# Last FFN projection of a decoder layer: lighter forms for three pairs, weight sums in two goes, another order at its start and its end

## The chip, the cores and the metric

The kernel runs on one core of a Trainium2 chip. The time is the device time of one execution in microseconds (us). TensorE (PE in the profile, PEld its weight loads) multiplies, VectorE (DVE) and ScalarE (ACT) work on the elements, GpSimd (POOL) helps, SyncE (SP) issues most transfers.

## The reference

One layer over 512 tokens of width 1024, in fp32:

```python
h = rms_norm(x, norm_mix)
q_a, k_a, v_a, u_b, gate_b, gate_c, g_a, g_b = split(h @ w_in)
o_a = stick_breaking_attention(q_a, k_a, v_a)           # 8 heads of 64, causal
y_b = gate_b * causal_depthwise_conv(gate_c * u_b, conv_w)
x = x + (sigmoid(g_a) * (o_a @ w_branch_a) + sigmoid(g_b) * (y_b @ w_branch_b)) @ w_mix_out
x = x + memory_cross_attention(rms_norm(x, norm_mem_q), rms_norm(mem, norm_mem_kv), ...)   # 256 memory tokens
gate, up = split(rms_norm(x, norm_ffn) @ w_ffn_in)      # 2 x 2816 columns
x = x + (silu(gate) * up) @ w_ffn_out
out = rms_norm(x, norm_final)
```

## The kernel before

Activations stand transposed, channels on the 128 partitions and tokens along the row. Every fp32 product is made of three fp32r products: a tile is split into a high part (an ACT cast, names ending in h) and the rest (a DVE subtraction, names ending in l), and TensorE adds high by high, high by rest and rest by high. A weight goes through `wr` (loaded), `wh` and `wl`.

The stages come one after another: input projection, attention and convolution, branches and merge (`merged`), the split of the memory; its keys (`km`, `kml`) and values (`vm`); the output projection of the mixer with its residual (`residual`, bank `r`, tiles `x1` and their gained split `x1g`); the memory attention; then the two FFN projections.

Both FFN projections use seven block products in place of eight (the Winograd form of Strassen's scheme). In the first one (`uses`, with bank names z, v and y), the tile m of the 22 hidden tiles gets products 0 to 6; `reads` and `second` bring them out of PSUM; `evict(m, 0..2)` multiplies by the scale `r2b`, takes the silu on ACT and writes the result into `acts[j]`, j being the pair of two hidden tiles, 11 in all (NJ), with two row blocks and two token halves in each.

The last projection (matmuls into `p`) needs per pair the forms of the activations, `forms[i, j]`, and of the weights, `ows[i, j]`, for i = 0 to 6. `act_first` makes forms 0 and 1 (cast f01h), `act_second` the forms 2 and 6 in one cast of 128x512 (f26h), form 3 (from n2) and t34, a 128x512 operation that prepares 4 and 5 in place; `act_third` makes 4 and 5 (f45h). The weights of products 0, 1 and 5 come from the matrix itself; those of 2, 3 and of 4, 6 are sums of its blocks, which POOL makes ahead, during the earlier stages: `weight_sums` loads a pair's four blocks (`pre`), adds four times, and stores the result to DRAM (`sums`). It starts behind `merged[1]`, whose element POOL copies first to be held back; its pool `prepool` must be closed before the FFN's pool `fpool` opens.

The projection runs in two loops. The first one makes products 0 to 3 of every pair: `run(i, j)` is product i of pair j, two token tiles of 128 with three matmuls each; between them `part()` takes the next entry of `first_parts`, which writes the casts and subtractions of a pair to come. Entries for the first two or three pairs are written inside the last products of the first projection. The second loop makes products 4, 6 and 5 and, in between, turns eight blocks of the residual (`turned`, `begin`, `onto`: `rt` and `nrt` are the scales by token and their negative). Then come the closing matmuls, the squares for the final norm (`square`), the multiplication by the gain (`gained` on POOL), `rstd` with `rstd_end` (a Newton step for the reciprocal root after Ln and Exp), and the stores.

On PE, ACT and DVE this part runs in the order in which it is written (`manual_schedule`); POOL and SP take their queues in order as well.

Of the kernel before, what the change touches and what calls it, by code (L numbers as in the profile page):

```python
# [34 lines left out]
SUMS_AT = 1  # L35

# [4 lines left out]
def hybrid_layer(ctx: ExitStack, tc: tile.TileContext, xT_d, memT_d, cols_d, wv_d, win_d,  # L41
# [414 lines left out]
    def weight_sums(prepool):  # L456

        for j in range(NJ):
            t = prepool.tile([P, 4, 512], F32, tag="pre", name=nm("pre"))
            if j < 2:  # L460
                nc.gpsimd.tensor_copy(t[:, 0, 0:1], f(merged[SUMS_AT][0])[:, 0:1])
            nc.gpsimd.dma_start(t, wfo_d[j])
            for a, b in ((0, 2), (2, 1), (1, 0), (3, 1)):
                nc.gpsimd.tensor_tensor(out=t[:, a, :], in0=t[:, a, :], in1=t[:, b, :], op=ALU.add)  # L464
# [129 lines left out]
    x1, x1g, mean1 = residual(wmix_d, merged, None, g_q)  # L594

# [205 lines left out]
    def act_first(j):  # L801
        for i, (hi, lo) in enumerate(zip(*map(halves, split(acts[j][0], "f01")))):
            forms[i, j] = hi, lo

    def act_second(j):

        n1, b22 = halves(acts[j][1])
        n2 = tmp("n2", HS)
        nc.vector.scalar_tensor_tensor(out=n2, in0=n1, scalar=-1.0, in1=b22, op0=ALU.mult,
                                       op1=ALU.subtract)  # L810
        for i, (hi, lo) in zip((2, 6), zip(*map(halves, split(acts[j][1], "f26")))):
            forms[i, j] = hi, lo
        hi, lo = halves(unit("f3"))
        nc.scalar.copy(hi, n2)
        nc.vector.tensor_tensor(out=lo, in0=n2, in1=f(hi), op=ALU.subtract)
        forms[3, j] = hi, lo
        b = acts[j][0].rearrange("p (i t) -> p i t", i=2)
        nc.vector.scalar_tensor_tensor(out=b, in0=n2[:, None, :].broadcast_to([P, 2, HS]),
                                       scalar=-1.0, in1=b, op0=ALU.mult, op1=ALU.subtract)

    def act_third(j):
        for i, (hi, lo) in zip((4, 5), zip(*map(halves, split(acts[j][0], "f45")))):
            forms[i, j] = hi, lo

    def out_pair(j, src, i0, i1):
# [4 lines left out]
        nc.scalar.copy(hi, raw)  # L830
        nc.vector.tensor_tensor(out=lo, in0=raw, in1=f(hi), op=ALU.subtract)  # L831
        for n, i in enumerate((i0, i1)):
            ows[i, j] = hi[:, n, :], lo[:, n, :]

    def out_one(j):
# [7 lines left out]
        nc.vector.tensor_tensor(out=w[:, 1, :], in0=raw, in1=f(w[:, 0, :]), op=ALU.subtract)  # L843
# [4 lines left out]

    first_parts = []
    for j in (0, 1):  # L850
        first_parts.append(lambda j=j: (out_pair(j, wq(j), 0, 1), act_first(j)))
    for j in (0, 1):
        first_parts.append(lambda j=j: (out_pair(j, sums[j][:, 0:2, :], 2, 3), act_second(j)))
    for j in range(2, NJ - 2):
        first_parts.append(lambda j=j: (out_pair(j, wq(j), 0, 1), act_first(j)))
        first_parts.append(lambda j=j: (out_pair(j, sums[j][:, 0:2, :], 2, 3), act_second(j)))
    for j in (NJ - 2, NJ - 1):
        first_parts.append(lambda j=j: (out_pair(j, wq(j), 0, 1), act_first(j)))
    for j in (NJ - 2, NJ - 1):
        first_parts.append(lambda j=j: (out_pair(j, sums[j][:, 0:2, :], 2, 3), act_second(j)))  # L860
# [5 lines left out]
    with tc.manual_schedule(engines={mybir.EngineType.PE, mybir.EngineType.Activation,  # L866
# [6 lines left out]
        for n, (m, i) in enumerate(uses):  # L873
# [36 lines left out]

# [20 lines left out]
        for j in (0, 1):  # L931
            run(0, j)
            part()
            run(1, j)
        res[3] = [ztile("p3") for _ in range(2)]
        res[2] = [otile("p2") for _ in range(2)]
        for j in (0, 1):
            run(2, j)
            part()
            run(3, j)  # L940
        for j in range(2, NJ - 2):
# [5 lines left out]
            run(3, j)  # L947
        last = NJ - 2, NJ - 1
# [13 lines left out]
        out_pair(0, sums[0][:, 2:4, :], 4, 6)  # L962
# [4 lines left out]
        out_pair(1, sums[1][:, 2:4, :], 4, 6)  # L967
        out_one(0)

        res[4], res[6] = [ztile("p4") for _ in range(2)], [mmtile("p6") for _ in range(2)]  # L970
        gain = [f(unit("gain")) for _ in range(2)]
        for h in range(2):
            nc.sync.dma_start(gain[h], gfin_d[:, h * 512:(h + 1) * 512].broadcast_to([P, 512]))
        ss = cpool.tile([P, 2 * TT], F32, tag="ss", name="ss")
# [46 lines left out]
        for j in range(NJ - 2):  # L1021
# [7 lines left out]
            out_pair(j + 2, sums[j + 2][:, 2:4, :], 4, 6)  # L1029
            if j > 0:  # L1030
# [6 lines left out]
        out_one(NJ - 1)  # L1037
        for s2 in range(2):
# [42 lines left out]
        def end(s2):  # L1081
            for j in range(NJ - 3, NJ):
                run(5, j, [s2])
            onto(ys[s2, 1], res[5][s2], s2, ys[s2, 1], -1)
            square(s2, 1)

        hi, t0, t1 = slice(2, 4), slice(0, 1), slice(1, 2)
        rstd(hi)
        end(0)
        rstd_end(hi)  # L1090
        store(2, 1, "act")
        store(2, 0, "dve")
        rstd(t0)
        end(1)
        store(3, 1, "act")
        rstd_end(t0)
        store(0, 1, "both")
        store(0, 0, "act")
        rstd(t1)
        store(3, 0, "dve")  # L1100
# [66 lines left out]
```

## Time and profile before

| | |
|---|---|
| three runs | 867.35, 867.08, 866.11 us (median 867.08) |
| the profiled execution | 869.89 us, its span 868.2 us |
| mean granted clock of TensorE | 0.993 |
| PE busy | 850.9 us, 98% of the span, 4840 matmuls |
| PEld busy | 739.7 us, 85% |
| DVE busy | 659.8 us, 76%, 1080 instructions |
| ACT busy | 460.5 us, 53%, 842 |
| POOL busy | 153.1 us, 18%, 183 |

A row of the timeline gives the start within the span and the duration in us, the engine and the line of the kernel, the operation with what it writes and reads (an arrow from the inputs to the output), the sizes, and in brackets how long the engine had been idle and what released it. The profiled execution is one of its own, 2.81 us above the median of the three runs, with 1.69 us lying outside its span; rows and sums of rows are measured against it.

### The profile page before, as it was taken

Reading aid. Unit: us, or ns where it says so; the run is one execution under the profiler, and the core shown is the slowest. Engines: PE = TensorE matmul, PEld = TensorE weight load, DVE = VectorE, ACT = ScalarE, POOL = GpSimd, SP = SyncE. Lnnn points to the kernel's source line nnn. Section 1 sums busy time; section 2 is a strip of 40 time slices with the busy share of each in tenths; the row PEclk is TensorE's granted clock in tenths of the full one; section 3 lists DMA queues with packets and bytes.
Section 4 is the critical chain, followed back from the end, with each engine's and each line's share of the span. In section 5 each row is a group of like instructions: output and inputs, shape, how many; then the busy total and the mean of one; then the engine's idle time right before and its main releaser. Section 6 shows DMA issues by size and latency. Waiting matters only on the chain.

```text
span 868.2 us, 12834 instructions
## 1 busy us (share of the span) xinstructions
PE 850.9 (98%) x4840; PEld 739.7 (85%) x4840; DVE 659.8 (76%) x1080; ACT 460.5 (53%) x842; POOL 153.1 (18%) x183
## 2 busy tenths in 40 slices
PE   9999999999999999999999999999999999899995
PEld 7878888887888888888888789999999999788884
DVE  7768888987665778656555679888778887798866
ACT  7566676775332344443344556644555555566545
POOL 0021221101666665100000001111111110000002
PEclk9999999999999999999999999999999999899998
DMA  8332222224677788733341435777777763365642
GB/s 292 121 110 85 85 64 70 77 76 165 229 282 294 283 317 315 243 97 97 121 111 49 108 75 140 177 183 183 182 193 185 183 170 107 102 225 190 212 136 97
DMA packets 48574, 139.54 MB, mean 161 GB/s; under 512 B 4608, under 2 KB 6656, under 8 KB 45696
## 3 DMA queue, kind: packets, MB, share of 16 engines
q1 hardware_dynamic: 39008, 103.82, 35.7%
q0 software_dynamic: 9216, 34.61, 15.5%
q8 instruction: 38, 0.62, 0.3%
q10 hardware_dynamic: 288, 0.28, 0.1%
q14 instruction: 24, 0.20, 0.1%
HBM read 125.07 MB, written 13.63 MB: 160 GB/s over the span
## 4 chain that ended last, share of the span: by engine, by line
PE 92%; DVE 4%; issue 2%; ACT 1%; DMA 1%; SPq 0%; POOL 0%; DVEq 0%; ACTq 0%; POOLq 0%
PE z L724 14%; PE p L919 10%; PE pr L151 8%; PE pr L152 8%; PE pr L153 8%; PE y L724 7%; PE v L724 4%; PE r L152 3%; PE r L151 3%; PE r L153 3%; PE v L257 2%; PE br L151 2%; PE mq L153 2%; PE mq L151 2%; PE mq L152 2%
## 5 line engine op out<-in xcount | busy, mean ns | idle before, releaser
L146 ACT CAST wh<-wr 128x1024 fp32r<-128x1024 f32 x84 | 88.1, 1052 | 159.0 <-issue 66.9
L147 DVE TENSOR_TENSOR wl<-wr,wh 128x1024 fp32r<-128x1024 f32 x84 | 116.2, 1387 | 34.5 <-ACT wh L146 34.3
L152 PE MATMUL pr<-xgl,wh 128*128 128x512 f32 x288 | 112.5, 390 | 0.0
L151 PE MATMUL pr<-xgh,wh 128*128 128x512 f32 x288 | 112.4, 390 | 0.0
L153 PE MATMUL pr<-xgh,wl 128*128 128x512 f32 x288 | 112.2, 390 | 0.0
L693 POOL DMA_DIRECT2D ws<-in_w_ffn_in_dram x22 | 26.5, 1206 | 315.3 <-DVE wf L714 113.9
L464 POOL TENSOR_TENSOR pre<-pre 128x512 f32<-128x512 f32 x44 | 71.5, 1629 | 29.2 <-DMA pre<-in_w_ffn_out_dram 26.9
L724 PE MATMUL z<-xdh,wf 128*128 128x256 f32 x352 | 70.5, 283 | 0.2 <-ACT sb L745 0.2
L153 PEld LDWEIGHTS pr<-xgh,wl 128*128 128x128 f32 x288 | 54.1, 188 | 11.4
L151 PEld LDWEIGHTS pr<-xgh,wh 128*128 128x128 f32 x288 | 54.1, 188 | 11.0
L152 PEld LDWEIGHTS pr<-xgl,wh 128*128 128x128 f32 x288 | 54.1, 188 | 10.9
L724 PEld LDWEIGHTS z<-xdh,wf 128*128 128x128 f32 x352 | 58.0, 192 | 0.5 <-ACT sb L745 0.4
L745 ACT COPY sa<-z 128x256 f32<-128x256 f32 x44 | 16.4, 373 | 78.9 <-PE z L724 78.0
L714 DVE TENSOR_TENSOR wf<-s,wf 128x512 fp32r<-128x512 f32 x44 | 30.3, 691 | 25.7 <-ACT wf L713 25.6
L724 PE MATMUL z<-xdl,wf 128*128 128x256 f32 x176 | 49.8, 283 | 0.0
L831 DVE TENSOR_TENSOR wl<-wr,wh 128x1024 fp32r<-128x1024 f32 x33 | 40.4, 1223 | 7.4 <-ACT wh L830 7.4
L830 ACT CAST wh<-wr 128x1024 fp32r<-128x1024 f32 x33 | 34.7, 1051 | 7.0 <-ACT f01h L165 3.7
L724 PE MATMUL z<-xch,wf 128*128 128x256 f32 x176 | 35.4, 284 | 0.1
L724 PE MATMUL y<-xch,wf 128*128 128x256 f32 x176 | 35.4, 283 | 0.0
L724 PE MATMUL v<-xoh,wf 128*128 128x256 f32 x176 | 35.4, 283 | 0.0
L724 PE MATMUL z<-xf,wf 128*128 128x256 f32 x264 | 35.4, 283 | 0.0
L724 PE MATMUL y<-xoh,wf 128*128 128x256 f32 x176 | 35.3, 283 | 0.0
(322 smaller groups left out, 2426.9 us busy)
## 6 DMA issues: line engine op xcount, KB each, us to landing
wr<-in_w_in_dram SPq DMA_DIRECT2D x36, 512.0 KB, 3.5
pre<-in_w_ffn_out_dram POOLq DMA_DIRECT2D x11, 1024.0 KB, 8.3
sums<-pre POOLq DMA_DIRECT2D x11, 1024.0 KB, 5.1
ws<-in_w_ffn_in_dram SPq DMA_DIRECT2D x22, 512.0 KB, 3.7
wg<-in_w_ffn_in_dram SPq DMA_DIRECT2D x22, 512.0 KB, 4.1
ws<-in_w_ffn_in_dram POOLq DMA_DIRECT2D x22, 512.0 KB, 6.0
wr<-sums SPq DMA_DIRECT2D x22, 512.0 KB, 4.2
wr<-in_w_ffn_out_dram SPq DMA_DIRECT2D x16, 512.0 KB, 3.7
```

Of the source, the lines that this page charges most:

```text
L146: after(nc.scalar.copy(h2, raw), lead[-1:])
L147: lows.append(nc.vector.tensor_tensor(out=l2, in0=raw, in1=f(h2), op=ALU.subtract))
L151: nc.tensor.matmul(ps, a[0], b[0], start=start, stop=False, **kw)
L152: nc.tensor.matmul(ps, a[0], b[1], start=False, stop=False, **kw)
L153: nc.tensor.matmul(ps, a[1], b[0], start=False, stop=stop, **kw)
L464: nc.gpsimd.tensor_tensor(out=t[:, a, :], in0=t[:, a, :], in1=t[:, b, :], op=ALU.add)
L693: nc.gpsimd.dma_start(s13, a[:, 0:4:3, :], accum_op=ALU.add)
L714: nc.vector.tensor_tensor(out=w[:, 1, :], in0=raw, in1=f(w[:, 0, :]), op=ALU.subtract)
L724: nc.tensor.matmul(ps[:, :HS], a, b, start=i < 3 and k == 0 and j == 0, stop=k == KP - 1 and j == 2, skip_group_check=True)
L830: nc.scalar.copy(hi, raw)
L831: nc.vector.tensor_tensor(out=lo, in0=raw, in1=f(hi), op=ALU.subtract)
L919: nc.tensor.matmul(res[i][s2], a[:, ts], b, start=j == 0 and n == 0, stop=j == NJ - 1 and n == 2)
```

## The change

It has four parts. For the first three pairs (`LIGHT`), `act_second` makes only forms 2 and 3, 128x256 each, with n2 in place; form 6 goes to `act_third`, and t34 is written into the first loop at pairs 5, 6 and 7. The casts and subtractions of pairs 0 and 1 are written apart from one another and among the last evictions of the first projection, and the table load goes from there to the start of the second loop. The weight sums are made in two goes: pairs 0 to 7 (`SUMS_FIRST`) where they were, pairs 8 to 10 behind the first residual tile `x1g[0]`, and `prepool` closes after that. At the end, `run(5, 7)` joins the closing matmuls (`BEHIND`), so that each token tile has twelve in place of nine; `out_one(10)` stands behind the four `onto`; the gain vector is scaled by -0.5 on ACT, which shortens `rstd_end`; POOL multiplies two blocks less by the gain, and the stores come in another order and form. The number of matmuls stays.

```diff
-    def weight_sums(prepool):
-        for j in range(NJ):
+    def weight_sums(some, behind):
+        for n, j in enumerate(some):
...
-            if j < 2:
-                nc.gpsimd.tensor_copy(t[:, 0, 0:1], f(merged[SUMS_AT][0])[:, 0:1])
+            if n < 2:
+                nc.gpsimd.tensor_copy(t[:, 0, 0:1], f(behind)[:, 0:1])
...
-            weight_sums(prepool)
+            weight_sums(range(SUMS_FIRST), merged[m][0])
...
-    prestack.close()
-    fpool = ctx.enter_context(tc.tile_pool(name="fpool", bufs=2))
...
     x1, x1g, mean1 = residual(wmix_d, merged, None, g_q)
+    weight_sums(range(SUMS_FIRST, NJ), x1g[0][0])
+    prestack.close()
+    fpool = ctx.enter_context(tc.tile_pool(name="fpool", bufs=2))
...
     def act_second(j):
+        if j < LIGHT:
+            rest_of(*half_form(2, j, 0))
+            n2_of(halves(acts[j][1])[0], j)
+            rest_of(*half_form(3, j, 0))
+            return
...
     def act_third(j):
...
+        if j < LIGHT:
+            rest_of(*half_form(6, j, 1))
...
             if (m, i) == (NF - 2, 6):
-                second(NF - 1)
                 evict(m, 0)
                 evict(m, 1)
+                x3 = half_form(3, 0, 0)
+                rest_of(*x3)
             if (m, i) == (NF - 1, 5):
                 evict(NF - 2, 2)
-            if n - len(uses) in (-6, -3, -1):
-                first_parts.pop(0)()
+                out_pair(*w23(0))
+                x2 = half_form(2, 1, 0)
+                rest_of(*x2)
+                n2_of(x2[0], 1)
+            if n == len(uses) - 6:
+                w, x = out_cast(*w01(0)), cast_first(0)
+                rest_of(*w)
+                rest_of(*x)
+            elif (m, i) == (NF - 1, 4):
+                w, x = out_cast(*w01(1)), cast_first(1)
+                rest_of(*w)
+                rest_of(*x)
+                x2 = half_form(2, 0, 0)
+                second(NF - 1)
+                rest_of(*x2)
+                n2_of(x2[0], 0)
         evict(NF - 1, 0)
         evict(NF - 1, 1)
-        tables = log_exp_tables(silus[-1])
+        x3 = half_form(3, 1, 0)
+        w = out_cast(*w23(1))
+        rest_of(*x3)
         evict(NF - 1, 2)
+        rest_of(*w)
...
             run(3, j)
+            if NJ - 2 - LIGHT <= j + 1 < NJ - 2 + 1:
+                n = j + 1 - (NJ - 2 - LIGHT)
+                if n < LIGHT:
+                    t34_of(n, halves(acts[n][1])[0])
...
+        tables = log_exp_tables(silus[-1])
         gain = [f(unit("gain")) for _ in range(2)]
         for h in range(2):
             nc.sync.dma_start(gain[h], gfin_d[:, h * 512:(h + 1) * 512].broadcast_to([P, 512]))
+            nc.scalar.activation(gain[h], gain[h], AF.Copy, scale=-0.5)
...
-            if j > 0:
+            if 0 < j < BEHIND + 1:
                 run(5, j - 1)
...
         for j in last:
             run(4, j)
-        out_one(NJ - 1)
...
             onto(ys[s2, 1], res[4][s2], s2, ys[s2, 1], -1)
+        out_one(NJ - 1)
...
             square(2 + s2, 0)
-            gained(2 + s2, 0)
...
-            nc.vector.tensor_tensor(out=a, in0=y, in1=y, op=ALU.mult)
-            nc.vector.scalar_tensor_tensor(out=a, in0=a, scalar=-0.5, in1=rv[:, ts], op0=ALU.mult,
-                                           op1=ALU.mult)
-            nc.vector.scalar_tensor_tensor(out=a, in0=a, scalar=1.5, in1=y, op0=ALU.add,
+            if ts.stop - ts.start == 1:
+                nc.vector.tensor_scalar(out=a, in0=y, scalar1=y, scalar2=rv[:, ts], op0=ALU.mult,
+                                        op1=ALU.mult)
+            else:
+                nc.vector.tensor_tensor(out=a, in0=y, in1=y, op=ALU.mult)
+                nc.vector.tensor_tensor(out=a, in0=a, in1=rv[:, ts], op=ALU.mult)
+            nc.vector.scalar_tensor_tensor(out=a, in0=a, scalar=-3.0, in1=y, op0=ALU.add,
                                            op1=ALU.mult)
...
-            for j in range(NJ - 3, NJ):
+            for j in range(BEHIND, NJ):
                 run(5, j, [s2])
...
-        store(2, 0, "dve")
+        square(0, 1)
+        store(2, 0, "both")
+        store(3, 0, "both")
+        store(3, 1, "act")
```

On POOL, where the sums of the last pairs are made (`pre` is loaded from the weights of the last projection, `sums` is the result in DRAM), there stands before, from the end of pair 7 on:

```order
L464 TENSOR_TENSOR pre_2429<-pre_2429 128x512 x3
L466 DMA sums_2435<-pre_2429 128x2048
L462 DMA pre_2437<-in_w_ffn_out_dram 128x2048
L462 DMA pre_2445<-in_w_ffn_out_dram 128x2048
L464 TENSOR_TENSOR pre_2437<-pre_2437 128x512 x4
L464 TENSOR_TENSOR pre_2445<-pre_2445 128x512
L466 DMA sums_2443<-pre_2437 128x2048
L464 TENSOR_TENSOR pre_2445<-pre_2445 128x512 x3
```

and now:

```order
L467 TENSOR_TENSOR pre_2429<-pre_2429 128x512 x3
L469 DMA sums_2435<-pre_2429 128x2048
L464 COPY pre_3894<-xgh_3598 128x1
L464 COPY pre_3903<-xgh_3598 128x1
L465 DMA pre_3894<-in_w_ffn_out_dram 128x2048
L465 DMA pre_3903<-in_w_ffn_out_dram 128x2048
L467 TENSOR_TENSOR pre_3894<-pre_3894 128x512 x4
L467 TENSOR_TENSOR pre_3903<-pre_3903 128x512
L469 DMA sums_3901<-pre_3894 128x2048
L467 TENSOR_TENSOR pre_3903<-pre_3903 128x512 x3
```

Pairs 8 to 10 now stand behind two copies from `xgh`, the split of the first residual tile.

On DVE at the passage from the first projection to the last (`a` is the tile of acts that an eviction writes, `fg` the gate of a hidden tile; L762 multiplies by r2b, L772 is the eviction, L831 a weight's rest, L809 n2, L818 t34), from the eviction of hidden tile 20 on, there stands before:

```order
L772 SCALAR_TENSOR_TENSOR a_7924<-sb_7635,fg_7671 128x256
L776 TENSOR_TENSOR a_7924<-a_7923,a_7924 128x256
L750 TENSOR_TENSOR fg_7801<-y_7821,sa_7762 128x256
L831 TENSOR_TENSOR wl_7944<-wr_7941,wh_7943 128x1024
L809 SCALAR_TENSOR_TENSOR n_7947<-a_5287 128x256
L166 TENSOR_TENSOR f26l_7950<-a_5287,f26h_7949 128x512
L815 TENSOR_TENSOR f_7953<-n_7947,f_7953 128x256
L818 SCALAR_TENSOR_TENSOR a_5286<-n_7947,a_5286 128x512
L762 TENSOR_TENSOR fg_7801<-fg_7801,r0b_5196 128x512
L772 SCALAR_TENSOR_TENSOR a_7923<-z_7761,fg_7801 128x256
L772 SCALAR_TENSOR_TENSOR a_7924<-sb_7763,fg_7801 128x256
L831 TENSOR_TENSOR wl_7975<-wr_7972,wh_7974 128x1024
```

and now, with L810 for every rest of a split, L831 for n2, L765 for the product with r2b and L775 for the eviction:

```order
L810 TENSOR_TENSOR fh_7917<-a_5289,fh_7917 128x256
L775 SCALAR_TENSOR_TENSOR a_7932<-z_7635,fg_7673 128x256
L775 SCALAR_TENSOR_TENSOR a_7933<-sb_7637,fg_7673 128x256
L779 TENSOR_TENSOR a_7933<-a_7932,a_7933 128x256
L810 TENSOR_TENSOR wl_7940<-wr_7937,wh_7939 128x1024
L810 TENSOR_TENSOR fh_7943<-a_5556,fh_7943 128x256
L831 SCALAR_TENSOR_TENSOR a_5556<-a_5556 128x256
L753 TENSOR_TENSOR fg_7803<-y_7823,sa_7764 128x256
L765 TENSOR_TENSOR fg_7803<-fg_7803,r0b_5198 128x512
L810 TENSOR_TENSOR fh_7962<-a_5556,fh_7962 128x256
L775 SCALAR_TENSOR_TENSOR a_7932<-z_7763,fg_7803 128x256
L775 SCALAR_TENSOR_TENSOR a_7933<-sb_7765,fg_7803 128x256
```

Between the last but one eviction and the last one, pair 0's f26l of 128x512 and its t34 are gone; n2 of pair 0 and form 2 of pair 0 have moved ahead of the first eviction, and forms 2 and 3 of pair 1, 128x256 each, stand between the two.

On DVE at the end (`wq` is the weight of product 5, `uv`, `u` and `elh` are blocks of the result that L977 completes, `rms` the final norm's scales), there stands before, from the last two weights of product 5 on:

```order
L843 TENSOR_TENSOR wq_8870<-wr_8828,wq_8870 128x512
L843 TENSOR_TENSOR wq_8887<-wr_8885,wq_8887 128x512
L977 SCALAR_TENSOR_TENSOR uv_8536<-p_8521,nrt,uv_8536 128x512
L977 SCALAR_TENSOR_TENSOR u_8506<-p_8521,nrt,u_8506 128x512
L977 SCALAR_TENSOR_TENSOR uv_8538<-p_8522,nrt,uv_8538 128x512
L977 SCALAR_TENSOR_TENSOR u_8508<-p_8522,nrt,u_8508 128x512
L977 SCALAR_TENSOR_TENSOR elh_8572<-p_8523,rt,elh_8572 128x512
L977 SCALAR_TENSOR_TENSOR elh_8649<-p_8524,rt,elh_8649 128x512
L1054 TENSOR_TENSOR rms<-ss 128x2
L1057 TENSOR_SCALAR rms<-rms 128x2
L977 SCALAR_TENSOR_TENSOR u_8506<-p_8540,nrt,u_8506 128x512
```

and now, with L810 for the rest of a split and L1056 for the completion:

```order
L810 TENSOR_TENSOR wq_8871<-wr_8835,wq_8871 128x512
L1056 SCALAR_TENSOR_TENSOR uv_8540<-p_8522,nrt,uv_8540 128x512
L1056 SCALAR_TENSOR_TENSOR u_8507<-p_8522,nrt,u_8507 128x512
L1056 SCALAR_TENSOR_TENSOR uv_8542<-p_8523,nrt,uv_8542 128x512
L1056 SCALAR_TENSOR_TENSOR u_8509<-p_8523,nrt,u_8509 128x512
L810 TENSOR_TENSOR wq_8898<-wr_8896,wq_8898 128x512
L1056 SCALAR_TENSOR_TENSOR elh_8579<-p_8524,rt,elh_8579 128x512
L1056 SCALAR_TENSOR_TENSOR elh_8656<-p_8525,rt,elh_8656 128x512
L1132 TENSOR_TENSOR rms<-ss 128x2
L1135 TENSOR_SCALAR rms<-rms 128x2
L1147 TENSOR_TENSOR rms<-rms 128x2
```

The last `wq` moved behind four completions, and the chain of `rms` lies ahead of the next completion as a whole.

More of the change, by code (lines that the diff above doesn't have):

```diff
@@ L799, in halves, with cast_of, rest_of, cast_half @@
         return t[:, :HS], t[:, HS:]
-    def act_first(j):
-        for i, (hi, lo) in enumerate(zip(*map(halves, split(acts[j][0], "f01")))):
-            forms[i, j] = hi, lo
-    def act_second(j):
+    def cast_of(src, s, cols=512):
+        hi, lo = unit(s + "h", cols), unit(s + "l", cols)
+        nc.scalar.copy(hi, src)
+        return src, hi, lo
+    def rest_of(src, hi, lo):
+        nc.vector.tensor_tensor(out=lo, in0=src, in1=f(hi), op=ALU.subtract)
+    def cast_half(src, s):
+        hi, lo = halves(unit(s))
+        nc.scalar.copy(hi, src)
+        return src, hi, lo
+    def pair_of(i, j, parts):
+        forms[i, j] = parts[1:]
+    def both_of(i0, i1, j, parts):
+        for i, hi, lo in zip((i0, i1), halves(parts[1]), halves(parts[2])):
+            forms[i, j] = hi, lo
+    def cast_first(j):
+        parts = cast_of(acts[j][0], "f01")
+        both_of(0, 1, j, parts)
+        return parts
+    def n2_of(out_, j):
         n1, b22 = halves(acts[j][1])
-        n2 = tmp("n2", HS)
-        nc.vector.scalar_tensor_tensor(out=n2, in0=n1, scalar=-1.0, in1=b22, op0=ALU.mult,
+        nc.vector.scalar_tensor_tensor(out=out_, in0=n1, scalar=-1.0, in1=b22, op0=ALU.mult,
                                        op1=ALU.subtract)
[L811 to L816, printed above, removed]
+    def t34_of(j, n2):
         b = acts[j][0].rearrange("p (i t) -> p i t", i=2)
@@ L830, in out_pair @@
         nc.scalar.copy(hi, raw)
-        nc.vector.tensor_tensor(out=lo, in0=raw, in1=f(hi), op=ALU.subtract)
         for n, i in enumerate((i0, i1)):
             ows[i, j] = hi[:, n, :], lo[:, n, :]
+        return raw, hi, lo
+    def out_pair(*args):
+        rest_of(*out_cast(*args))
     def out_one(j):
@@ L932, in hybrid_layer @@
             run(0, j)
-            part()
             run(1, j)
@@ L936, in hybrid_layer @@
         res[2] = [otile("p2") for _ in range(2)]
+        part()
         for j in (0, 1):
             run(2, j)
+            run(3, j)
             part()
-            run(3, j)
         for j in range(2, NJ - 2):
@@ L961, in hybrid_layer @@
         l1 = [plus("l1", res[1][s2], s0[s2]) for s2 in range(2)]
-        out_pair(0, sums[0][:, 2:4, :], 4, 6)
+        out_pair(*w46(0))
         act_third(1)
```

58 lines of the change are left out of this document (39 added, 19 removed).

## The prediction

> **What bounds the kernel now.** I read the chain of waits first, then TensorE's waits grouped by releaser, then TensorE's timeline wherever a wait was large. The page's chain (share of the span by engine) and two groups of waits (us in all, how many, the longest):
>
> ```profile
> PE 92%; DVE 4%; issue 2%; ACT 1%; DMA 1%; SPq 0%; POOL 0%; DVEq 0%; ACTq 0%; POOLq 0%
> ...
> PE km L151 <- DVE km L518: 2.6, 4, 0.8
> ...
> PE p L919 <- ACT f26h L165: 1.4, 1, 1.4
> ```
>
> TensorE carries the end, and the change leaves its number of matmuls alone. Time can only come from matmuls that start late or run at a lower clock, and from the tail. Three places qualify: the keys of the memory (km), the passage from the first FFN projection to the last (p), and the end. At the passage the timeline shows (start, duration, engine, line, idle time before it and its releaser):
>
> ```profile
> 743.57 0.40 PE L919 MATMUL p<-wh,f01h 128*128 128x512 f32 x1
> ...
> 749.04 0.39 PE L919 MATMUL p<-wh,f26h 128*128 128x512 f32 x1
> ...
> 751.96 0.50 PE L919 MATMUL p<-wh,f 128*128 128x512 f32 x1 [0.72 <-DVE a L772]
> ...
> 754.37 0.79 PE L919 MATMUL p<-wh,f26h 128*128 128x512 f32 x1 [1.44 <-ACT f26h L165]
> ...
> 756.05 0.80 PE L919 MATMUL p<-wh,f26l 128*128 128x512 f32 x1
> ...
> 760.49 0.51 PE L919 MATMUL p<-wh,f01h 128*128 128x512 f32 x1
> ```
>
> From 743.57 to 749.04 stand 24 matmuls, 0.228 apart. The next 24 should take 5.47 and reach product 0 of pair 2 at about 754.5; it starts at 760.49, 6.0 late. Part is waiting, part the doubled durations, since the clock falls there. The windows (busy us and count of PE, PEld, DVE, ACT, POOL, then the granted clock):
>
> ```profile
> 750.47:753.89 3.42, 1.75 (x7) 0.80 (x5) 1.12 (x4) 3.05 (x4) 0.00 (x0) 1.00 0.25 93
> 753.80:753.90 0.10, 0.00 (x0) 0.00 (x0) 0.07 (x1) 0.10 (x2) 0.00 (x0) 0.93 0.00 0
> 760.70:760.80 0.10, 0.10 (x1) 0.09 (x1) 0.10 (x2) 0.10 (x1) 0.00 (x0) 0.94 0.94 369
> 856.28:859.69 3.41, 2.13 (x10) 1.44 (x8) 3.17 (x9) 1.64 (x5) 1.56 (x2) 1.00 0.00 0
> 863.10:863.20 0.10, 0.00 (x0) 0.00 (x0) 0.09 (x1) 0.00 (x0) 0.00 (x0) 0.56 1.11 430
> ```
>
> The 0.93 puts the fall to 0.50 at 753.89, the 0.94 the return at 760.71, the 0.56 the last fall at 863.11. 760.71 less 753.89 is 6.82, twice 3.41; 863.11 less 760.71 is 102.40, thirty times 3.413: changes lie on a fixed grid. A grid window with 1.67 us of idle TensorE (1.75 busy of 3.42) was answered with half clock; one with 1.28 idle (2.13 of 3.41) was not. The matmul at 756.05 is the last that waited (its f26l ends then); the ten starts from there to 760.49 would take 2.3 at 0.228, so at full clock product 0 of pair 2 would have begun at 758.4: 3.9 of the 6.0 is waiting, 2.1 is clock.
>
> **The change, part by part.** *Sums taken out of the km stage.* The stage, 192 matmuls, and what lies beside it:
>
> ```profile
> 313.21 0.28 PE L151 MATMUL km<-mgh,wh 128*128 128x256 f32 x1
> ...
> 339.99 0.40 PE L151 MATMUL vm<-wh,mgh 128*128 128x512 f32 x1
> ```
> ```profile
> 318.90 8.61 POOL L464 TENSOR_TENSOR pre<-pre 128x512 f32<-128x512 f32 x5 [3.03 <-DMA pre<-in_w_ffn_out_dram]
> ```
> ```profile
> 328.52 1.52 DVE L523 TENSOR_TENSOR kml<-km,kmh 128x256 fp32r<-128x256 f32 x1
> 330.29 1.96 DVE L147 TENSOR_TENSOR wl<-wr,wh 128x1024 fp32r<-128x1024 f32 x1
> ...
> 335.08 0.41 DVE L523 TENSOR_TENSOR kml<-km,kmh 128x256 fp32r<-128x256 f32 x1
> ```
>
> It takes 26.78; 192 matmuls at 0.12 are 23.0, so 3.8 are lost. While POOL adds, the same subtraction takes 1.52, without it 0.41; TensorE then waits for a bank of km, 2.6 in the group above. In the changed order these adds (pairs 8 and 9) go. The gain lies between the 2.6 of the group and the 3.8; I take 3.3, nearer the stage's own loss because stalls between short matmuls are not all listed.
>
> *The sums put behind the first residual tile.* The third tile of that stage on DVE:
>
> ```profile
> 378.30 0.69 DVE L575 TENSOR_TENSOR x<-r,x 128x512 f32<-128x512 f32 x1 [2.04 <-PE r L153]
> 379.20 1.23 DVE L147 TENSOR_TENSOR wl<-wr,wh 128x1024 fp32r<-128x1024 f32 x1 [0.21 <-ACT wh L146]
> 380.34 0.75 DVE L169 SCALAR_TENSOR_TENSOR xgl<-x,gcol,xgh 128x512 fp32r<-128x512 f32 x1
> 381.00 0.69 DVE L591 TENSOR_TENSOR acc<-acc,sq 128x512 f32<-128x512 f32 x1
> ```
>
> A tile is 24 matmuls, 5.44, of which DVE works 3.36. Two periods earlier (367.4, and 1.5 for the split) the first xg is there and POOL's queue opens; with some 10 for the loads, eight adds of 1.6 and a store, its adds lie at about 379 to 392 and again near 400. With the growth of the two rows above (1.1 for the smaller operations, 0.75 for wl) DVE needs 3.36+1.1+1.1+0.75 = 6.3 per 5.44, a lag of 0.9 per tile, 2.2 over 13 us. TensorE has another bank: DVE may be late by 5.44 less 0.69, 4.7. Cost between 0 and rival B's 2.7; I take 0. The next pool opens only after these stores, and its first load was issued late:
>
> ```profile
> 428.40 0.33 SPq L690 DMA_DIRECT2D a<-in_w_ffn_in_dram  x1
> ```
>
> Pool work ends about 408, 20 us ahead. On POOL itself the first loads of FFN weights stand behind the sums, and have the same 20 us.
>
> *The passage.* Casts and subtractions of pairs 0 and 1 move ahead of the last evictions, the form of product 6 and the 128x512 t34 leave. The paces of DVE's operations, and the present end of the eviction:
>
> ```profile
> 747.09 1.22 DVE L831 TENSOR_TENSOR wl<-wr,wh 128x1024 fp32r<-128x1024 f32 x1
> 748.22 0.42 DVE L809 SCALAR_TENSOR_TENSOR n<-a 128x256 f32<-128x256 f32 x1
> 748.56 0.68 DVE L166 TENSOR_TENSOR f26l<-a,f26h 128x512 fp32r<-128x512 f32 x1
> ...
> 749.16 0.42 DVE L815 TENSOR_TENSOR f<-n,f 128x256 fp32r<-128x256 f32 x1
> ...
> 751.48 0.43 DVE L772 SCALAR_TENSOR_TENSOR a<-z,fg 128x256 f32<-128x256 f32 x1 [0.70 <-ACT fg L764]
> ```
> ```profile
> 739.45 0.37 ACT L745 COPY sb<-z 128x256 f32<-128x256 f32 x1 [1.04 <-PE z L724]
> ...
> 750.81 0.63 ACT L764 ACTIVATE fg<-fg 128x512 f32<-128x512 f32 x1 [1.73 <-DVE fg L762]
> ```
>
> Start to start that is 1.13 for wl, 0.60 for 128x512, 0.34 (0.46 where the next waits) for 128x256. Walked through in the new order from pair 1's wl at 740.8 (ACT's copy of z ends at 739.8, the cast wh before that wl takes 1.04): 1.14+0.60+0.34+0.46+0.34+0.46+0.68 brings the product fg by r2b to 744.8; ACT's silu and the half cast to 745.9; the eviction, pair 0's weight subtraction, two halves and the second fg to 750.4; the last silu and half cast to 751.4. The a from the z bank ends at 752.17, against 751.91 now: product 3's second matmul tile starts at 752.22 where 751.08 would be ideal, 1.14 late. The last weight subtraction begins at 752.4, its consumer starts at 753.69, 0.56 late. What vanishes is the wait for the 128x512 f26h. So product 0 of pair 2 begins at 754.5+1.14+0.56 = 756.2, 4.3 before the present 760.49, if the clock stays: idle 0.98 and 0.40 in the records make 1.38 within 2.45 us, between the 1.28 that was let pass and the 1.67 that was not, and only in (3.41-2.45)/3.41 = 28% of the grid's positions does one window hold both. Bounds: 2.2 (waits alone) and 6.0 (all). I take 4.3.
>
> [...]
>
> *The first loop* gains t34 at pairs 5, 6 and 7, 0.60 each on DVE:
>
> ```profile
> 778.28 1.23 DVE L831 TENSOR_TENSOR wl<-wr,wh 128x1024 fp32r<-128x1024 f32 x1 [0.60 <-ACT wh L830]
> ```
>
> DVE idles 0.60 in each 5.44 there; the cover is just as large as the work, and the forms are made a pair ahead. Cost 0, bound 0.6.
>
> *The start of the second loop.* ACT gets the table load and two scalings of gain, which wait for its transfer; their issue and the time to landing (min, median, max):
>
> ```profile
> 807.28 0.90 SPq L973 DMA_DIRECT2D gain<-in_gain_final_dram  x2
> ...
> DMA to landing us min/median/max: 4.4/4.5/4.6
> ```
>
> Gain lands by 811.9. Behind two scalings (0.63 each by the row of a 128x512 ACT operation above) f45h of pair 2 starts at 813.2; with its 0.6, wh's 1.04, a hop of 0.3 and wl's 1.22 the weights are there at 816.4 (estimate), 1.1 before TensorE would take them at 817.5. Cost 0, and past the 1.1 it is rival D.
>
> *The end.* Twelve closing matmuls each instead of nine; more of TensorE's work covers the chain of u.
>
> ```profile
> 848.73 0.39 PE L919 MATMUL p<-wh,f45h 128*128 128x512 f32 x1
> ```
> ```profile
> 848.75 1.21 DVE L831 TENSOR_TENSOR wl<-wr,wh 128x1024 fp32r<-128x1024 f32 x1
> ...
> 859.74 0.74 DVE L977 SCALAR_TENSOR_TENSOR u<-p,nrt,u 128x512 f32<-128x512 f32 x1
> ...
> 863.50 0.75 DVE L1076 SCALAR_TENSOR_TENSOR u<-u,rms,gain 128x512 f32<-128x512 f32 x1
> ```
>
> Six matmuls (1.36) fewer stand ahead of the last products 4, but their weights wait for the wl at 848.75: 1.05 comes back as a stall. The last wq's subtraction now stands behind four ontos and a cast, some 1.5 later than it could be; the shorter rstd_end takes 0.2 to 0.3 from each chain, and three "both" stores replace POOL's gain. Walked through, the last store starts at 864.2 to 864.9 instead of 863.5. Cost 0.65, bounds -0.7 (all of the shorter chain shows) and +1.2.
>
> **Sum.** -3.3 - 4.3 + 0.65 = -7.0. The profiled execution took 869.89; it becomes 862.9. It stands 2.8 above the median 867.08; against that I forecast 860.2.
>
> **The rivals.** *A: the clock falls in the changed kernel too.* One grid window at half clock costs 1.7, two 3.4: 861.9 to 863.6. For it: 1.38 idle lies close to 1.67. Against: 28%. *B: the moved sums stall the residual stage.* If each of the three operations waits for a whole POOL add, 8.61/5 = 1.72, DVE needs 3.36+5.16 = 8.5 per 5.44, lags 3.1 a tile, 7.4 over 13 us, and 2.7 show past the 4.7: 862.9. Against: 1.52 is the longest the small one took. [...] *C: the passage isn't shortened*, because evictions end later than now (752.17 against 751.91) and the forms hang on them: 867.08-3.3+0.65 = 864.4. *D, the slower side: gain lands late.* Every cast of the second loop stands behind it on ACT. 7.0 of gain and 1.7 of measurement are used up when it lands 1.1+8.7 later than 4.5, at 14 us after issue. Loads of the sums show landings up to 11.3:
>
> ```profile
> DMA to landing us min/median/max: 4.2/6.4/11.3
> ```
>
> At 11.3 it would be 865.9, at 14 868.8.
>
> **How the numbers follow.** A measurement tells about 0.2%, 1.7 us, from no change: faster is under 865.35. Forecast 0.60, A 0.14, B 0.07, C 0.10, D 0.09. C's spread of 1.5 puts 0.04 of its 0.10 within 0.2%; D gives 0.04 same and 0.05 slower. Faster 0.60+0.14+0.07+0.06 = 0.87, same 0.08, slower 0.05. The forecast's own range is 857.8 (km 3.8, passage 4.7, end -0.7) to 862 (2.6, 3.8, +1.2). The whole range goes to 864.5 for A, B and half of C; left out are D, the rest of C and some 0.05 below.
>
> **What would show it.** Km stage at 23 to 24 us with kml at 0.41; no wait for r beyond a few tenths; product 0 of pair 2 some 12.6 after the first p, without "f26h" among its releasers, clock 1.00; no wait of TensorE at about product 4 of pair 2; a stall of about 1 before the last products 4; last store 0.7 later against the last matmul's place. Wrong would make it: a fall of the clock elsewhere, or new waits for r, for p in the first loop, or for gain.

## The result, and the profile after

The changed kernel took 862.04 us (median of four, 861.54 to 862.60) against 867.22 for the kernel before on that chip: a ratio of 0.9943, 95% interval 0.9926 to 0.9960. A second series gave 862.08 against 867.72, ratio 0.9929 (0.9917 to 0.9942). By the two ratios the change is worth 4.9 and 6.2 us, where 6.9 was forecast (867.08 to 860.2); by the medians it is 5.2 and 5.6.

The profiled execution of the changed kernel took 862.09, its own median almost to the digit; the profiled execution of before had stood 2.8 above its median. Between the two profiles lie 7.8 us, between the medians 5.2. What the profiles show comes first. The chain of waits of the changed kernel, and TensorE's waits by releaser:

```profile
PE 95%; DVE 3%; ACT 1%; issue 1%; POOL 0%; ACTq 0%; DVEq 0%; POOLq 0%
...
PE p L992 <- DVE wl L810: 1.1, 2, 0.9
PE y L727 <- DVE sb L758: 0.7, 1, 0.7
```

The waits for km (2.6), for f26h (1.4) and for the a of the last eviction (0.7) are gone; a wait for y and one for two weight rests are new. The km stage and the passage on TensorE:

```profile
312.82 0.28 PE L154 MATMUL km<-mgh,wh 128*128 128x256 f32 x1
...
336.10 0.40 PE L154 MATMUL vm<-wh,mgh 128*128 128x512 f32 x1
...
739.08 0.39 PE L727 MATMUL y<-xoh,wf 128*128 128x256 f32 x1 [0.73 <-DVE sb L758]
...
740.62 0.40 PE L992 MATMUL p<-wh,f01h 128*128 128x512 f32 x1
...
749.69 0.50 PE L992 MATMUL p<-wl,fh 128*128 128x512 f32 x1 [0.27 <-DVE wl L810]
...
752.34 0.39 PE L992 MATMUL p<-wh,f01h 128*128 128x512 f32 x1
...
841.69 0.50 PE L992 MATMUL p<-wl,f45h 128*128 128x512 f32 x1 [0.86 <-DVE wl L810]
```

The km stage takes 23.28 in place of 26.78. From the first p to product 0 of pair 2 it is 11.72 in place of 16.92, and a window over the end of the passage (busy us of PE, PEld, DVE, ACT, POOL, then the granted clock) has the clock at 1.00, where before it stood at 0.50 from 753.89 to 760.71. It falls nowhere ahead of 856, near the end of the span:

```profile
748.00:756.00 8.00, 7.73 (x34) 5.88 (x33) 6.96 (x11) 5.71 (x9) 0.00 (x0) 1.00 0.56 195
```

In the residual stage, DVE beside POOL's adds; then the last store, and the gain vector's wait on ACT:

```profile
374.20 9.16 POOL L467 TENSOR_TENSOR pre<-pre 128x512 f32<-128x512 f32 x5 [6.88 <-DMA pre<-in_w_ffn_out_dram]
```
```profile
374.41 0.69 DVE L575 TENSOR_TENSOR x<-r,x 128x512 f32<-128x512 f32 x1 [2.05 <-PE r L156]
...
376.50 1.77 DVE L172 SCALAR_TENSOR_TENSOR xgl<-x,gcol,xgh 128x512 fp32r<-128x512 f32 x1
378.19 1.78 DVE L591 TENSOR_TENSOR acc<-acc,sq 128x512 f32<-128x512 f32 x1
...
385.69 0.68 DVE L575 TENSOR_TENSOR x<-r,x 128x512 f32<-128x512 f32 x1
...
855.86 0.75 DVE L1159 SCALAR_TENSOR_TENSOR u<-u,rms,gain 128x512 f32<-128x512 f32 x1
```
```profile
803.69 1.26 ACT L1052 ACTIVATE gain<-gain 128x512 f32<-128x512 f32 x2 [1.59 <-DMA gain<-in_gain_final_dram]
```

The operations beside the adds grow by 1.0 to 1.1 (0.75 to 1.77, 0.69 to 1.78), but DVE has 2.05 idle there: the x of two tiles later starts at 385.69, 0.4 behind two periods of 5.44 (374.41 + 10.88 = 385.29). The next one, at 390.73, is back in step. TensorE never waits for r; its stage lasts 43.29 from first r to last, as before.

### The profile page after: what moved, and what is told of

The parts are those of the page before. It is cut to its first block, busy times and chain, and to the rows that moved or that the text cites. A ratio compares the mean times of both kernels' runs of the same rounds, so it can differ in the third digit from the quotient of the medians.

```text
span 860.4 us, 12842 instructions
## 1 busy us (share of the span) xinstructions
PE 846.9 (98%) x4840; PEld 737.6 (86%) x4840; DVE 656.9 (76%) x1082; ACT 460.2 (53%) x846; POOL 152.2 (18%) x183
## 4 chain that ended last, share of the span: by engine, by line
PE 95%; DVE 3%; ACT 1%; issue 1%; POOL 0%; ACTq 0%; DVEq 0%; POOLq 0%
PE z L727 15%; PE p L992 9%; PE pr L155 8%; PE pr L154 8%; PE pr L156 8%; PE y L727 7%; PE v L727 4%; PE r L155 3%; PE r L156 3%; PE r L154 3%; PE v L260 3%; PE br L154 2%; PE mq L156 2%; PE br L155 2%; PE mq L155 2%; PE mq L154 2%
## 5 line engine op out<-in xcount | busy, mean ns | idle before, releaser
L150 DVE TENSOR_TENSOR wl<-wr,wh 128x1024 fp32r<-128x1024 f32 x84 | 110.4, 1316 | 36.7 <-ACT wh L149 36.6
L810 DVE TENSOR_TENSOR wl<-wr,wh 128x1024 fp32r<-128x1024 f32 x33 | 40.3, 1223 | 4.7 <-ACT wh L877 4.7
```

What stands on the lines that cost most here:

```text
L150: lows.append(nc.vector.tensor_tensor(out=l2, in0=raw, in1=f(h2), op=ALU.subtract))
L810: nc.vector.tensor_tensor(out=lo, in0=src, in1=f(hi), op=ALU.subtract)
```

## The experiments

Each kernel was timed beside the kernel before, in three groups: the first four experiments on one chip (before 867.92, 23 runs), the next four (867.72, 9 runs) and the last four (868.08, 20 runs) on another.

**The parts alone.** *Sums in two goes* on the kernel before:

```diff
-            weight_sums(prepool)
+            weight_sums(range(SUMS_FIRST), merged[m][0])
...
     x1, x1g, mean1 = residual(wmix_d, merged, None, g_q)
+    weight_sums(range(SUMS_FIRST, NJ), x1g[0][0])
+    prestack.close()
```

> The kernel before with the weight sums in two goes and nothing else. Theory 1 (the adds of pairs 8 to 10 slowed the km stage and cost nothing where they stand now): the km stage from first km to first vm shrinks from 26.8 to 23.3 us, the residual stage keeps its length, the time falls by 3.5 to about 863.7. Rival (POOL's adds slow DVE as much at the new place): the residual stage grows by 2 or more and the time falls by 1.5 or less, to 865.7 or above.

865.60, ratio 0.9979 (0.9967 to 0.9990): 1.8 faster, 0.9 to 2.9. In its profile the km stage takes 23.30 and the residual stage 43.30: the place is as theory 1 has it and the rival's longer residual stage did not come, but the 3.5 of the profile is more than the timed runs gave. Why they gave less is open. The passage, unchanged in this kernel, had its clock at half for 3.4 only (753.2 to 756.6; the window 753.40 to 756.40 is at 0.50) and took 16.03, against 16.92 with 6.8 before:

```profile
739.65 0.40 PE L921 MATMUL p<-wh,f01h 128*128 128x512 f32 x1
...
755.68 0.63 PE L921 MATMUL p<-wh,f01h 128*128 128x512 f32 x1
```

*The passage* (light forms, order, table load) with the old sums and the old end:

```diff
-SUMS_FIRST = 8
+SUMS_FIRST = 11
...
-            if 0 < j < BEHIND + 1:
+            if j > 0:
                 run(5, j - 1)
```

> The changed kernel with the sums in one go and the old end: only the light forms and the passage in its new order are left. Theory 1a (the 2.1 us at half clock that the profile of before shows at the passage are in its timed runs too): 4.4 faster, 862.8. Theory 1b (the profiled execution had them, most timed ones had less): 2.3 to 3 faster, 864.2 to 864.9, and the granted clocks of the runs of before lie above the 0.993 of its profile. Both: a wait of 0.7 for the bank y just ahead of the last product of the first projection.

863.64, ratio 0.9956 (0.9942 to 0.9971): 3.8 faster, 2.5 to 5.0. The interval holds the 4.4 of theory 1a and also the upper part of theory 1b's 2.3 to 3.0. Its runs show clocks of 0.996 to 0.997 beside 0.992 to 0.996 of before, and 13 of those 23 lie above the 0.993 of the profile, as 1b had it. The clock is a mean over the span and takes in the fall at its end, so it is no measure of the passage alone. Between 1a and 1b these runs do not decide; the wait of 0.7 for y is there.

*The end* with the scaled gain on the kernel before:

```diff
-            if j > 0:
+            if 0 < j < BEHIND + 1:
                 run(5, j - 1)
...
+            nc.scalar.activation(gain[h], gain[h], AF.Copy, scale=-0.5)
```

> The kernel before with the new end and the scaled gain vector alone. Theory 1 (a stall of about 1 ahead of the last products 4, repaid only in part by a shorter chain): 0.65 slower, 867.9. Rival (the shorter chain of the final norm wins): 0.5 or more faster, 866.7 or less.

868.52, ratio 1.0010 (0.9998 to 1.0022): 0.9 slower, the interval from 0.2 faster to 1.9 slower. The sign alone is not settled by the time, but a gain of 0.5 is outside. The profile shows the wait of 0.9 for a weight rest ahead of the last products 4. The three parts sum to 1.8 + 3.8 - 0.9 = 4.7, close to the 4.9 of the first comparison of the whole.

**The wait for y.**

```diff
                 w, x = out_cast(*w01(1)), cast_first(1)
+                second(NF - 1)
                 rest_of(*w)
                 rest_of(*x)
                 x2 = half_form(2, 0, 0)
-                second(NF - 1)
```

> The changed kernel with one DVE addition (second of the last hidden tile, which frees the bank y) written ahead of pair 1's two subtractions in place of behind them. Theory 1 (TensorE's wait of 0.73 for y, 0.84 start to start, came from that place): the wait goes, 0.6 to 0.84 faster than the changed kernel, about 861.3. Rival (DVE's queue at the passage is the bound, so the time turns up as a longer wait for the last weight rest): no change, 862.0.

861.71 on a chip where the changed kernel itself wasn't run (ratio to before 0.9934, 0.9919 to 0.9949). In the profile the wait for y is gone and the first p comes 0.95 sooner after vm, but the passage grows from 11.72 to 12.36. Of its waits, the one for a is new:

```profile
PE p L992 <- DVE wl L810: 1.1, 2, 0.9
PE p L992 <- DVE a L775: 0.6, 1, 0.6
```

In the profile the rival is right for two thirds: 0.64 of the 0.95 comes back as a longer passage, so DVE's queue was the next bound, and 0.3 is left.

**Sums back in one go, beside the changed kernel.** The changed kernel again, and with SUMS_FIRST = 11:

> The changed kernel once more, as the reference for the three others. Theory 1 (the shares measured one by one add up: 2.1 from the sums, 3.9 from the passage, 1.0 back at the end): 5.0 below the kernel before in the timed runs. Rival (the whole 7.8 between the two profiled executions is real, and the first comparison caught fast runs of before): 7 or more below.

> The changed kernel with all weight sums in one go again, where they were. Theory 2 (the profiled execution of a kernel with POOL's adds in the km stage loses more there than its ordinary executions do): the profile shows the km stage at 26.3 to 26.8, some 3.3 longer than the changed kernel, and is the slowest of its runs or close to it, while the median of the timed runs lies only about 2.1 above the changed kernel. Rival (the profile tells the true size, and the 2.1 of the first comparison was chance): 3.3 above in the timed runs as well.

862.08 (ratio 0.9929) and 864.87 (ratio 0.9960, 0.9945 to 0.9974). The sums are worth 2.8 in these medians, between the 2.1 of theory 2 and the 3.3 of its rival. The profile of the second:

```profile
312.80 0.28 PE L154 MATMUL km<-mgh,wh 128*128 128x256 f32 x1
...
339.08 0.40 PE L154 MATMUL vm<-wh,mgh 128*128 128x512 f32 x1
```

That is 26.28, 3.0 more than 23.28, and its execution (865.01) was the third of five, not the slowest. So for this kernel theory 2's sign, a profile slower than the ordinary runs, is missing. The five runs lie at 863.20, 864.17, 864.87, 865.01 and 866.07 at clocks of 0.997 and 0.998, the changed kernel's five between 861.37 and 862.41: a spread of 2.9 with the adds beside the km stage and of 1.0 without. That the adds make the spread is not shown: the kernel with the passage alone has them too and spreads by 1.6 in six runs, and the one with the sums alone, without them, by 3.7 in twelve. The 5.0 expected for the changed kernel was 5.6 by the medians, the 7 of its rival at the end of the interval (5.0 to 7.2).

**What the passage consists of.** The light forms alone on the kernel before (act_second with forms 2 and 3 for three pairs, form 6 in act_third, t34 in the loop):

```diff
+        if j < LIGHT:
+            half_form(2, j, 0)
+            nc.vector.scalar_tensor_tensor(out=n1, in0=n1, scalar=-1.0, in1=b22, op0=ALU.mult,
+                                           op1=ALU.subtract)
+            half_form(3, j, 0)
+            return
```

> The kernel before with only the light forms of the first three pairs: forms 2 and 3 alone in the passage, form 6 with forms 4 and 5, t34 in the first loop; order, table load, sums and end as before. Theory 1 (the order of the writing and the moved table load carry most of the passage's 3.9, since ACT's queue of silu, table load and casts sets the late form): 0.5 to 1.5 faster than before, the wait for the second token half's bank and a wait for the first form of pair 1 remain, and the clock still falls in the profile. Rival (the work left out is what shortens it): 3 or more faster, no wait for a form.

867.00, ratio 0.9987 (0.9978 to 0.9996): 1.1 faster, as theory 1 said; that ACT's queue sets the late form was not tried by itself. The passage takes 15.33 (741.98 to 757.31), 0.7 less than the 16.03 of the sums alone, which had 3.4 at half clock as well. The new order and the moved table load were not run alone; they get the rest of the gain only by subtraction. The waits stay, the longest under another name, and the clock is at half once, for 3.4:

```profile
PE p L940 <- ACT fh L809: 1.2, 1, 1.2
PE p L940 <- DVE a L773: 0.5, 1, 0.5
```
```profile
752.80:756.20 3.40, 2.94 (x8) 2.34 (x8) 2.38 (x5) 2.09 (x4) 0.00 (x0) 0.51 0.42 146
```

*Filling matmuls* in the two waits of the kernel before:

```diff
+    zero = cpool.tile([P, P], F32, tag="zero", name="zero")
+    zr = cpool.tile([P, P], F32R, tag="zr", name="zr")
+    nc.gpsimd.memset(zero, 0.0)
+    nc.gpsimd.tensor_copy(zr, zero)
...
+        def fill(n):
+            for _ in range(n):
+                nc.tensor.matmul(res[0][0][:, :HS], zr, forms[0, 1][0], start=False,
+                                 stop=False)
...
+            if j == 1:
+                fill(12)
             run(2, j)
             part()
-            run(3, j)
+            if j == 0:
+                run(3, j, [0])
+                fill(6)
+                run(3, j, [1])
+            else:
+                run(3, j)
```

> The kernel before with 6 and 12 matmuls of 256 columns with zero weights (0.12 us each) in TensorE's two waits at the passage (they add nothing to the result); every other instruction as before. Theory 1 (the idle time lets the clock fall there, and about 2.1 of the timed runs' loss is half clock): the granted clock stays 1.00 through the passage, product 0 of pair 2 begins about 14.8 after the first p in place of 16.9, 1.7 to 2.1 faster than before, granted clocks of the runs at 0.996 to 0.998. Rival (the clock's fall is not TensorE's idling): the clock falls all the same, no gain.

866.61, ratio 0.9981 (0.9972 to 0.9990): 1.6 faster, 0.9 to 2.4, with 18 matmuls more. The passage lasts 14.88, at clock 1.00 throughout:

```profile
743.13 0.40 PE L923 MATMUL p<-wh,f01h 128*128 128x512 f32 x1
...
750.68 0.87 PE L928 MATMUL p<-f01h,zr 128*128 128x256 f32 x6
...
752.32 1.59 PE L928 MATMUL p<-f01h,zr 128*128 128x256 f32 x12
...
758.01 0.39 PE L923 MATMUL p<-wh,f01h 128*128 128x512 f32 x1
```
```profile
752.00:760.00 8.00, 7.30 (x36) 5.60 (x35) 6.61 (x10) 5.49 (x9) 0.00 (x0) 1.00 0.32 102
```

The runs' clocks are 0.996 and 0.997, those of before beside them 0.993 to 0.996. That the waits of 0.72 and 1.44 made the clock fall is shown by this: DVE and ACT do what they did, in the same order, and TensorE's idling is taken away but for two waits of 0.24 and 0.43. In the profile the fall costs 2.04 of the passage's 6 (16.92 to 14.88) where it lasts 6.8; where it lasts 3.4, as in the run with the sums alone, it is 1.15 (16.03 to 14.88).

**Further on the same road.** Two places where the changed kernel still waits, then both, then fewer pairs at the end:

```diff
+        w = out_cast(*w23(1))
         evict(NF - 1, 1)
+        rest_of(*w)
         x3 = half_form(3, 1, 0)
-        w = out_cast(*w23(1))
-        rest_of(*x3)
         evict(NF - 1, 2)
-        rest_of(*w)
+        rest_of(*x3)
```

> The changed kernel with a new order at the passage: second ahead of pair 1's subtractions as in the early-second run, the cast of pair 1's summed weights ahead of the last silu, its subtraction while DVE waits for that silu, and the last eviction ahead of the last half form. Theory 1 (DVE's queue, idle twice for 0.99 while ACT makes silu and half cast, is the bound there): product 0 of pair 2 begins about 11.0 after the first p in place of 11.72, and the first p 0.84 earlier: 1.3 to 1.5 faster than the changed kernel. Rival (the wait for the z bank is set by the silu's chain and only changes its name): at most 0.4 faster.

860.53 (ratio 0.9915, 0.9901 to 0.9928), 1.55 below the changed kernel's 862.08 of the same group. The first p comes 1.0 sooner after vm, the passage takes 11.50 (11.0 expected): the z bank still costs 0.3.

```diff
             run(4, j)
+        out_one(NJ - 1)
         for s2 in range(2):
...
-        out_one(NJ - 1)
...
-        store(3, 0, "both")
-        store(3, 1, "act")
         rstd(t0)
+        store(3, 1, "act")
+        rstd_end(t0)
         end(1)
         square(1, 1)
-        rstd_end(t0)
         store(0, 1, "both")
         rstd(t1)
-        store(0, 0, "dve")
+        store(0, 0, "act")
+        store(3, 0, "both")
```

> The changed kernel with another end: the last weight of product 5 ahead of the four completions again (its cast in ACT's idle time), and the blocks of the first two token tiles completed ahead of the stores of the others. Theory 1 (DVE's and ACT's queues set the end, with last weights late by 0.64 of waiting and a subtraction stretched to 1.37, and with u behind 1.41 of stores): the last store starts 1.3 to 1.7 earlier against the changed kernel, and the time falls as much. Rival (the volume of DVE's work after the last matmul sets the end, so the order is worth little): 0.5 or less.

860.82 (ratio 0.9917, 0.9903 to 0.9930), 1.26 below. From the start of the last matmul to the start of the last store it is 3.56 (850.61 to 854.17) in place of 4.95 (850.91 to 855.86).

```profile
850.61 0.39 PE L992 MATMUL p<-wq,f45l 128*128 128x512 f32 x1
```
```profile
854.17 0.75 DVE L1159 SCALAR_TENSOR_TENSOR u<-u,rms,gain 128x512 f32<-128x512 f32 x1
```

> The changed kernel with the new passage of the passage2 run and the new end of the tail2 run together. Theory 1 (they lie at different places): gains of 1.3 and 1.1 add up, 859.6. Rival (the end's chain takes up part of it): 860.2 or more.

859.67, ratio 0.9900 (0.9884 to 0.9915): the gains all but add up. This version beats both kernels; it lies 2.4 below the changed one's 862.08, a median of the group before.

```diff
-BEHIND = 7
+BEHIND = 8
```

> The same, with the number of pairs that close behind the loop back at three (product 5 of pair 7 in the loop). Theory 1 (the 1.02 stall ahead of the last products 4 goes, and TensorE's end with the new order sets the last store): 0.5 to 1.0 faster than the run before it, 858.8. Rival (the completions, 0.4 later than with four pairs behind, set it): 0.3 or less faster, or slower.

859.50 (ratio 0.9900, 0.9886 to 0.9914), no difference. The wait ahead of the last products 4 is gone and the last matmul starts at 847.95 in place of 849.72, yet the last store starts 113.69 after the first p as against 113.66: the completions set the end, as the rival says. On DVE the completion of the second token tile (`u` from p) starts 1.8 after the start of the last matmul (849.76 to 847.95), with four pairs behind 0.6 (850.33 to 849.72). So the stall of 1.0 that the changed end brings is not what the time is made of there; the chain of completions, squares and scales on DVE and ACT is.

## Why the prediction was right or wrong

*The sums.* Forecast 3.3; the profile shows 3.5 (26.78 to 23.28). The residual stage was to take them at no cost and does, with a lag of 0.4 where 2.2 was estimated: the growth per operation was right (1.1), but the adds cover only part of the operations and each period has its 2 idle. Rival B did not come about. In timed runs, however, this term is 1.8 (0.9 to 2.9) on the kernel before and 2.8 on the changed one. Whether ordinary executions lose less in the km stage than the profiled ones is open.

*The passage.* Forecast 4.3; in the profile it is 5.20 shorter, and 0.94 of that is lost just ahead of it (from the first vm to the first p it is 404.52 in place of 403.58), 4.26 in all; 3.8 in timed runs. The waits and the clock went as forecast, and rival A did not come about in any of the nine profiles that have the new passage. The 28% set against it took every position of the grid as equally likely; that was my assumption, and no run shows it (the last fall stands at 856.34 and 856.40 in the two profiles of the changed kernel). That 4.26 meets 4.3 so closely is in part luck, since two details were wrong and cancel. The 1.14 for the z bank isn't there, because the first p itself came later; where the wait for y is taken away, 0.60 of it appears. And the wait for y was missed: my walk through DVE began at pair 1's weight subtraction and never asked who waits for the addition that had been moved behind it. DVE's rows have it:

```profile
736.86 1.22 DVE L810 TENSOR_TENSOR wl<-wr,wh 128x1024 fp32r<-128x1024 f32 x1 [1.05 <-ACT wh L877]
738.00 0.69 DVE L810 TENSOR_TENSOR f01l<-a,f01h 128x512 fp32r<-128x512 f32 x1
738.60 0.42 DVE L758 TENSOR_TENSOR sb<-y,sb 128x256 f32<-128x256 f32 x1
```

DVE stood idle for 1.05 ahead of that subtraction, with the addition ready behind it: in the run with the addition written first it ran in that gap, 0.94 ahead of the subtraction (735.20 to 736.14).

*The first loop* cost 0 as forecast (51.68 from product 0 of pair 2 to the first xt, before 51.82). *The second loop:* ACT waited 1.59 for gain, TensorE not at all; rival D did not come about, its landing was 4.4 to 4.5. The hop of 0.3 in the estimate of 816.4 is shown by no row; DVE's row at 778.28 starts 0.04 after ACT's cast of wh has ended (777.19 and 1.05).

*The end.* The stall forecast at 1.05 measured 1.02 (840.44 to 841.69 start to start, less the ordinary 0.23). Counted from the first xt, the last store stands at 51.84 (804.02 to 855.86) against 51.19 (812.31 to 863.50): 0.65 later, as forecast, and 0.9 (-0.2 to 1.9) in timed runs.

*The step that failed* is the last one: "It stands 2.8 above the median 867.08; against that I forecast 860.2". The sum made against the profiled execution gave 862.9, and the measured times are 862.0 and 862.1. I took the 2.8 for a fixed distance between profiled and timed executions. It is none: both profiled executions of the changed kernel (862.09 and 862.16) lie within 0.1 of their medians, those of the eleven other kernels between 0.75 below and 1.67 above theirs. Among the 52 runs of before that later stood beside the experiments the highest is 869.92, so the profiled 869.89 was an extreme one.

Part of the 2.8 lay in what the change takes away. The 17 of those runs whose clock is 0.993, as in the profile, average 868.55, the 25 at 0.995 average 867.62. These 0.9 are about what 6.8 at half clock cost more than 3.4 at the passage (16.92 against 16.03); as most timed runs left no trace, that this is what parts them is argued and not shown. The km stage, 26.78 in this profile, is 26.14 to 26.79 in the six traces that have the adds beside it; against the 26.28 of three of them it adds 0.5. The stretch ahead of it, which the change leaves alone, ends anywhere from 312.05 to 313.34 in the fourteen traces, here at 313.21, some 0.4 behind their middle. By this estimate about 1 of the 2.8 is without a place, and for it the cause is open. What a change removes cannot keep its distance to the median; as far as the 2.8 was such time, subtracting it counted it twice.

Between the two profiles lie 7.8 where the sum has 7.0. The terms account for 7.1 (3.50 + 4.26 - 0.65); 0.4 is the earlier start of the km stage (312.82 against 313.21), which no term could foresee. The forecast of 860.2 was 1.8 too low. The measured 862.04 is at the end of the forecast's own range (to 862); that it lies well inside the whole range, which goes to 864.5, is luck, since that room was left for rivals A, B and C and none of them came about.

## What to carry to other kernels

A sum made from one profiled execution predicts an execution of the changed kernel: before it is set against the median, ask whether the execution lost its extra time in the very places that the change removes, and if so leave the distance out. When instructions are moved in an in-order queue, write down for each one that now stands later who waits for it, not only what the moved ones gain. Here waits of TensorE of 0.72 and 1.44 cost another 1.15 to 2.04 through the clock; whether waits do so in another kernel can be tried by filling them with matmuls that add zero.

## What the runs showed of the hardware

The clock's fall at the passage has no fixed length: the profiles show half clock for 6.8 us in the kernel before (753.89 to 760.71), for at least 6.4 in the run with the new end alone (0.50 from 754.20 to 760.60), for 3.4 in those with the sums alone (753.2 to 756.6) and the light forms alone (0.51 from 752.80 to 756.20), and none once the waits were filled (1.00 from 752 to 760). From one change of the clock to the next it is 6.82 and 102.40 in the profile of before, and 3.41 and 102.40 in that of the light forms, where windows of 0.2 put the changes at 752.86, 756.27 and 858.67. Gaps of 0.72 and 1.44 sufficed for the fall in this kernel, and filling them kept the clock at 1.00.

The same adds on POOL that cost TensorE 2.9 to 3.5 in the profiled km stages (26.14 to 26.79 against 23.28) cost it nothing in the residual stage (43.29 with and without them), though DVE's operations grow as much: there DVE needs 3.4 of each 5.44 without the adds. In the km stage a bank is 24 matmuls, 2.9, and beside the adds DVE took 3.66 from one bank of km to the next:

```profile
326.30 0.41 DVE L518 TENSOR_TENSOR km<-km,rmb 128x256 f32<-128x256 f32 x1
...
329.96 0.41 DVE L518 TENSOR_TENSOR km<-km,rmb 128x256 f32<-128x256 f32 x1
```

These rows show one thing more. This multiplication reads the bank of km in PSUM and only its second input from SBUF, and it takes 0.41 with the adds beside it as without (0.41 at 335.41); the subtraction behind it, with both inputs in SBUF, took 1.52 beside them (328.52) and 0.41 without (335.08). In the residual stage x, which reads the bank r, stayed at 0.69 in the same way (374.41 and, in the profile of before, 378.30). Why the adds lengthen the one and not the other is shown by no run.
